# Merging laced with dense matmuls, buffers of their own for the modulation weights, gathered transposes and a root per kind of token in a hybrid attention and delta-rule block

## The chip, the cores and the metric

The kernel runs on one core of a Trainium2 chip. The metric is the device time of one execution in microseconds; before the change the median of 3 runs is 1303.28 us (1297.49 to 1310.15). Less is better.

## The reference

Two layers (`DEPTH = 2`) act on 256 latent tokens and 256 context tokens of width 1024, in 32-bit floats. Each layer computes a mixer, a residual LayerNorm, an MLP with squared ReLU, and another residual LayerNorm:

```python
sh1, sc1, g1, sh2, sc2, g2 = split((silu(c) @ w_ada[l] + b_ada[l])[:, None, :], 6)
y_lat, y_ctx = token_mixer(x_lat * (1 + sc1) + sh1, x_ctx * (1 + csc1) + csh1, w_in[l], ...)
x_lat = layer_norm(ALPHA * x_lat + g1 * y_lat, ...)
x_lat = layer_norm(ALPHA * x_lat + g2 * squared_relu_mlp(x_lat * (1 + sc2) + sh2, ...), ...)
# token_mixer: half of the width is neighbourhood attention (8 heads of 64), half gated DeltaNet (4 heads of 128)
q, k = l2norm(q), l2norm(k);  q, k = rope_2d(q), rope_2d(k);  q = q * 128 ** -0.5
# gated_delta_chunked, per chunk of tokens, head and direction
a = where(strict, (kb @ k^T) * decay, 0);  tinv = unit_lower_inverse(a)
u = tinv @ (v * beta);  w = tinv @ (kb * exp(g));  attn = (q @ k^T) * decay
v_new = u - w @ s;  o = (q * exp(g)) @ s + attn @ v_new;  s = s * cd + k_dec^T @ v_new
# gated_rmsnorm
o = o * rsqrt(mean(o * o) + 1e-6) * w * silu(z)
```

The last layer returns the latent tokens alone. `o` is linear in `q`, so a factor of the query's token can be left out of `q` and be put into `o` and into the mean of its squares.

## The kernel before

Every product with a weight is done as three matmuls of split operands (`mm3`, lines 274 to 276: hi by hi, lo by hi, hi by lo). A weight block of 128x1024 comes by DMA into a raw buffer (`wraw`, four of them), ScalarE casts it to its hi part (line 248), VectorE subtracts that from it for the lo part (line 250); three blocks are made ahead.

The modulation (adaLN) is computed in steps (`ada_steps`): each loads a block of `w_ada` into one of the same raw buffers and multiplies it by the conditioning vector in four column strips (line 301, tile `adaps`).

The mixer of a layer (`mixer`) does, in this order: four DeltaNet heads (`gdn_head`: convolution of the projected queries, keys and values, rotation, l2 norm, transposes), the gates (`gates1`, `gates2`), then per 128-token tile `t` the matrix `U` of decayed key products (line 816); eight such 128x128 matrices (two directions, four heads) per tile, 32 in all. Their unit triangular inverses are found in three stages. *Elimination:* the diagonal 32x32 blocks of all 32 matrices are brought to the layout `MY` by four strided transposes on VectorE (line 824), one sign change on ScalarE (line 825), and 30 steps of a multiplication and a subtraction on VectorE (lines 831 and 833). *Tail:* a transpose (line 834), four strided copies on ScalarE to `XT` (836) and four strided transposes on VectorE to `U` (838). *Merge:* 32x32 blocks are merged to 64x64 by the products `p1` and `pz` (lines 849 to 856), these to 128x128 by `p2` and `p3` (lines 862 to 871), in two halves of 16 matrices. The products are 32x32 and 64x64 tiles of the array. Then the scan over four token tiles and two directions follows (`scan_step`; its first product is `pvn`, line 896), and the output norm of each tile (`o_stage`).

Neighbourhood attention shares the engines: projections `N`, `K`, `Q` and `Z` (tiles `psv`, `psn`, `psz`), and `attend` (scores and values in `pss`, softmax on VectorE and ScalarE). The strings `CFG["ord0"]` and `CFG["ord1"]` give the order in which these are written for each layer: `H` a head, `B` and `C` the gates, `N K Q Z` a projection of one block, `a` one tile of attention, `f` two steps of the modulation, and `X` the place where elimination, merge and scan are written. The framework's scheduler takes instructions out of the written order by their readiness and priority, and by the buffers of each pool, so the order on an engine differs from the one written.

Of the kernel before, what the change touches and what calls it, by code (L numbers as in the profile page):

```python
# [16 lines left out]
ALU = mybir.AluOpType  # L17
# [14 lines left out]
NHOLD = 6  # L32
NB0 = 3
# [7 lines left out]
    "ord0": "HHBHHCXfNffffNNfffffNKQffaaaKaQfaaKfaQfaffaaKfaQfaZaaaZZfffafffZ",  # L41
    "ord1": "BHHHHCNfffXNfffNfNfKfQfaafKfQfaaKfQKfaQfaafffZZZaZ", "tr": 7, "tr2": 2, "acc": 2, "g": 3, "n": 3,
# [134 lines left out]
def body(ctx, tc, a, out, dump=None):  # L177
# [289 lines left out]
    def mixer(l, hT, pre, ctx_m):  # L467
# [72 lines left out]

        def gdn_head(h):
            ss = small([128, 2, 4], "gss")
            rs = small([128, 2, 4], "grs")
            tk = {}
            if last:
                V.memset(ss, 1.0)
            for kind in (0, 1):
                pt, q0 = gdn_conv(h, kind)
                tk[kind] = ktok[h] if kind == 0 else ar("qtok").rearrange("p (t c) -> p t c", t=4)
                S.activation(tk[kind][:, q0:], pt[:, q0:], AF.Copy)  # L550
                sq = ar("gsq").rearrange("p (t c) -> p t c", t=4)
                S.activation(sq[:, q0:], pt[:, q0:], AF.Square)
                V.tensor_reduce(ss[:, kind, q0:], sq[:, q0:], axis=AX.X, op=ALU.add)
                x_ = tk[kind][:, 2:4]
# [9 lines left out]
            for kind in (0, 1):  # L564
                q0 = 2 if last and kind else 0
                x_ = tk[kind][:, q0:]
                V.tensor_tensor(x_, x_, rs[:, kind, q0:].unsqueeze(2).to_broadcast([128, 4 - q0, 128]), op=ALU.mult)
                pb = sm("gtb").rearrange("p (t c) -> p t c", t=4)
                for t in range(q0, 4):
                    PE.transpose(pb[:, t], tk[kind][:, t], ident)  # L570
# [10 lines left out]
        def proj_nv(hp):  # L581
            w = getw("w_vz", l, 0, hp)
            ps = proj_T(w, 0, "psv")
# [44 lines left out]
        def gates2():  # L628
            nonlocal gc, gx, gt, cd, eg, ngc, gcb, neg, kd
            pc = sm("pc")  # L630
# [102 lines left out]
        def proj_qk(hp, kind):  # L733
            if not kind:
                biases[hp] = load_bias(hp)
            w = getw("w_na", l, 2 * hp + kind)
            t0 = 256 if (last and kind) else 0
            ps = proj_T(w, t0, "psn")
# [30 lines left out]

        def run_order(o):  # L770
            for c in o:
                if c in "fBC":
                    {"f": fill, "B": gates1, "C": gates2}[c]()
                    continue
# [33 lines left out]

        for t in ts:
# [10 lines left out]
        q4 = [slice(32 * b, 32 * b + 32) for b in range(4)]  # L820
        MY = M.tile([128, 2, 32, 32], F32, name="MY", tag="my")
        MT, Y = MY[:, 0], MY[:, 1]
        for b in range(4):
            V.transpose(MT[q4[b]], U[q4[b], :, q4[b]].rearrange("p n i -> p i n"))
# [16 lines left out]
        for t2 in range(2):  # L841
            n0 = 16 * t2
            y1 = tr("y1").rearrange("p (n c) -> p n c", n=16)
            p1 = sm("p1").rearrange("p (n c) -> p n c", n=16)
            pz = sm("pz").rearrange("p (n c) -> p n c", n=16)
            A_, B_ = [slice(64 * r, 64 * r + 32) for r in range(2)], [slice(64 * r + 32, 64 * r + 64) for r in range(2)]
            for r in range(2):
                for n in range(16):
                    PE.matmul(p1[B_[r], n], U[A_[r], n0 + n, B_[r]], XT[A_[r], n0 + n, A_[r]], start=True, stop=True)
                S.activation(y1[B_[r]], p1[B_[r]], AF.Copy)  # L850
            for r in range(2):
                for n in range(16):
                    PE.matmul(pz[A_[r], n], y1[B_[r], n], U[B_[r], n0 + n, B_[r]], start=True, stop=True)
                    PE.matmul(pz[B_[r], n], U[B_[r], n0 + n, B_[r]], y1[B_[r], n], start=True, stop=True)
                V.tensor_scalar(U[A_[r], n0:n0 + 16, B_[r]], pz[A_[r]], -1.0, None, op0=ALU.mult)
                S.activation(XT[B_[r], n0:n0 + 16, A_[r]], pz[B_[r]], AF.Copy, scale=-1.0)
            lo_, hi_ = slice(0, 64), slice(64, 128)
            for t in (2 * t2, 2 * t2 + 1):
                n0 = 8 * t
                p2 = sm("p2").rearrange("p (n c) -> p n c", n=8)  # L860
                for n in range(8):
                    PE.matmul(p2[hi_, n], U[lo_, n0 + n, hi_], XT[lo_, n0 + n, lo_], start=True, stop=True)
                y2 = tr("y2").rearrange("p (n c) -> p n c", n=8)
                S.activation(y2[hi_], p2[hi_], AF.Copy)
                p3 = sm("p3").rearrange("p (n c) -> p n c", n=8)
                for n in range(4):
                    PE.matmul(p3[lo_, n], y2[hi_, n], U[hi_, n0 + n, hi_], start=True, stop=True)
                    PE.matmul(p3[hi_, 4 + n], U[hi_, n0 + 4 + n, hi_], y2[hi_, 4 + n], start=True, stop=True)
                V.tensor_scalar(U[lo_, n0:n0 + 4, hi_], p3[lo_, 0:4], -1.0, None, op0=ALU.mult)
                S.activation(XT[hi_, n0 + 4:n0 + 8, lo_], p3[hi_, 4:8], AF.Copy, scale=-1.0)  # L870
                V.tensor_tensor(U[:, n0 + 4:n0 + 8], XT[:, n0 + 4:n0 + 8],
                                beta[:, t, 4:8].unsqueeze(2).to_broadcast([128, 4, 128]), op=ALU.mult)
        if l == 0:
            dump("LT", U)
# [46 lines left out]
        def o_stage(t):  # L921
# [45 lines left out]
        for step in range(4):  # L967
            for d in range(2):
                scan_step(step, d)
# [148 lines left out]
    P0.tile([128, 40], F32, name="pad")  # L1118
# [194 lines left out]
```

## Time and profile before

| | |
|---|---|
| median of 3 runs | 1303.28 us (1297.49 to 1310.15) |
| the profiled execution | 1304.05 us, span 1302.3 us |
| mean granted clock of TensorE | 0.963 |
| busy: TensorE, its weight loads, VectorE, ScalarE, GpSimd | 95%, 77%, 67%, 46%, 6% of the span |

The profile gives an engine's busy time in a stretch, the time of one instruction by line and shape, what ended an engine's idle time, and the granted clock as a share of 2.4 GHz (0.50 is 1.2 GHz). A matmul's record is longer than the distance to the next one, since matmuls are pipelined. A 32-bit matmul of small tiles leaves two records per instruction.

### The profile page before, as it was taken

To read this page: it belongs to the slowest core of one execution; us is meant where nothing else is said; L and a number is where in the kernel's file an instruction comes from. 1 tells how busy PE (TensorE), PEld (TensorE's weight loads), DVE (VectorE), ACT (ScalarE), POOL (GpSimd) and SP (SyncE) were. 2 spreads that over 40 slices of the span, in tenths; PEclk is the share of its full clock that TensorE was granted. 3 is DMA by queue.
4 is the path that set the end of the run, shared out by engine and by line. 5 is a ranking of instruction groups with operands and counts; after the bars stand their busy time and mean duration, and the time that the engine had idled before them with its cause. 6 is when DMAs were issued, how large, how long until landed. Compare 5 with 4: busy or idle time off the path is not lost.

```text
span 1302.3 us, 20475 instructions
## 1 busy us (share of the span) xinstructions
PE 1234.8 (95%) x7976; PEld 1006.3 (77%) x7976; DVE 875.1 (67%) x1681; ACT 604.6 (46%) x1079; POOL 81.6 (6%) x82
## 2 busy tenths in 40 slices
PE   7999998999999999999999999899979998999997
PEld 3676666988878988777788888675669877788996
DVE  3788695466579955344444488897965668866677
ACT  2554545565555732322322455555454655544552
POOL 0212100001001000000000001221000010000000
PEclk9999995899999999999999999999958999899999
DMA  9613661023255643533532256235720256555552
GB/s 329 213 65 102 211 219 46 17 78 117 79 194 182 225 150 109 165 130 115 164 129 99 97 178 204 72 107 191 235 92 14 85 179 231 199 184 191 186 187 98
DMA packets 62721, 190.93 MB, mean 147 GB/s; under 512 B 7808, under 2 KB 17824, under 8 KB 62624
## 3 DMA queue, kind: packets, MB, share of 16 engines
q1 hardware_dynamic: 62624, 189.62, 44.2%
q8 instruction: 63, 1.03, 0.3%
q14 instruction: 34, 0.28, 0.1%
HBM read 187.46 MB, written 2.13 MB: 146 GB/s over the span
## 4 chain that ended last, share of the span: by engine, by line
PE 71%; DVE 11%; ACT 4%; issue 2%; POOL 1%; DMA 1%; DVEq 0%; ACTq 0%; POOLq 0%
PE pst L274 7%; PE pst L276 7%; PE pst L275 7%; PE pm L274 7%; PE pm L276 7%; PE pm L275 7%; PE pss L716 3%; PE adaps L301 2%; DVE wlo L250 2%; PE pss L696 2%; PE pss L713 2%; PE psn L274 1%; PE psn L275 1%; PE psn L276 1%; ACT XT L836 1%
## 5 line engine op out<-in xcount | busy, mean ns | idle before, releaser
L250 DVE TENSOR_TENSOR wlo<-wraw,whi 128x1024 fp32r<-128x1024 f32 x224 | 274.7, 1228 | 184.7 <-ACT whi L248 184.3
L248 ACT ACTIVATE whi<-wraw 128x1024 fp32r<-128x1024 f32 x224 | 237.0, 1060 | 316.6 <-PE pst L276 168.9
L274 PE MATMUL pm<-hhi,whi 128*128 128x256 f32 (+1 forms) x544 | 176.4, 324 | 0.8 <-ACT whi L248 0.7
L276 PE MATMUL pm<-hhi,wlo 128*128 128x256 f32 (+1 forms) x544 | 174.5, 321 | 0.0
L275 PE MATMUL pm<-hlo,whi 128*128 128x256 f32 (+1 forms) x544 | 174.4, 321 | 0.0
L274 PE MATMUL pst<-whi,ah 128*128 128x512 f32 x384 | 150.0, 391 | 0.0
L275 PE MATMUL pst<-wlo,ah 128*128 128x512 f32 x384 | 149.5, 389 | 0.0
L276 PE MATMUL pst<-whi,al 128*128 128x512 f32 x384 | 149.1, 389 | 0.0
L274 PEld LDWEIGHTS pm<-hhi,whi 128*128 128x128 f32 x544 | 103.5, 190 | 14.4 <-issue 5.8
L276 PEld LDWEIGHTS pm<-hhi,wlo 128*128 128x128 f32 x544 | 103.6, 190 | 7.7
L275 PEld LDWEIGHTS pm<-hlo,whi 128*128 128x128 f32 x544 | 103.6, 190 | 7.3
L274 PEld LDWEIGHTS pst<-whi,ah 128*128 128x128 f32 x384 | 72.1, 188 | 15.6 <-issue 0.8
L276 PEld LDWEIGHTS pst<-whi,al 128*128 128x128 f32 x384 | 72.1, 188 | 14.8
L275 PEld LDWEIGHTS pst<-wlo,ah 128*128 128x128 f32 x384 | 72.1, 188 | 14.7
L274 PE MATMUL psg<-hhi,whi 128*128 128x512 f32 (+1 forms) x216 | 78.2, 363 | 4.6 <-ACT XT L529 2.3
L276 PE MATMUL psg<-hhi,wlo 128*128 128x512 f32 (+1 forms) x216 | 78.0, 362 | 0.2 <-DVE wlo L250 0.2
L275 PE MATMUL psg<-hlo,whi 128*128 128x512 f32 (+1 forms) x216 | 77.8, 361 | 0.0
L531 DVE SCALAR_TENSOR_TENSOR XT<-U,cw,XT 128x512 f32<-128x512 f32 (+1 forms) x96 | 66.9, 728 | 0.5 <-ACT XT L529 0.4
L1191 ACT ACTIVATE ah<-mr 128x256 fp32r<-128x256 f32 (+1 forms) x68 | 33.5, 492 | 65.6 <-DVE mr L1189 65.6
L301 PE MATMUL adaps<-wraw,scT 128*32 128x256 f32 x640 | 56.0, 397 | 4.8 <-DMA wraw<-w_ada 4.6
L229 POOL TENSOR_TENSOR rs<-ve,mh 128x1 f32<-128x1 f32 x12 | 12.5, 1044 | 629.3 <-DVE bmv L394 362.2
L1192 DVE TENSOR_TENSOR al<-mr,ah 128x256 fp32r<-128x256 f32 (+1 forms) x68 | 35.2, 518 | 24.3 <-ACT ah L1191 24.2
(659 smaller groups left out, 2467.4 us busy)
## 6 DMA issues: line engine op xcount, KB each, us to landing
wraw<-w SPq DMA_DIRECT2D x140, 512.0 KB
wraw<-w_ada SPq DMA_DIRECT2D x80, 512.0 KB
wraw<-w_gdn SPq DMA_DIRECT2D x27, 512.0 KB
wraw<-w_out SPq DMA_DIRECT2D x24, 512.0 KB
xa<-w_ada SPq DMA_DIRECT2D x32, 256.0 KB
wraw<-w_vz SPq DMA_DIRECT2D x16, 512.0 KB
wraw<-w_na SPq DMA_DIRECT2D x16, 512.0 KB
lnrow<-lnr SPq DMA_DIRECT2D x8, 512.0 KB
```

The costliest lines, as they stand in the source:

```text
L248: S.activation(hi, r, AF.Copy)
L250: V.tensor_tensor(lo, r, hi.bitcast(F32), op=ALU.subtract)
L274: PE.matmul(o, l[0], r[0], start=start, stop=False)
L275: PE.matmul(o, l[0], r[1], start=False, stop=False)
L276: last_mm[:] = [PE.matmul(o, l[1], r[0], start=False, stop=stop).ins]
L301: PE.matmul(st["ps"][32 * g:32 * g + 32, :256], scT[:, k, :], w[:, 256 * g:256 * g + 256], start=(k == 0), stop=(k == 7), tile_position=(0 ...
L531: V.scalar_tensor_tensor(av, cin[:, sg:, kk:kk + 256], cw[:, b, kk:kk + 1], av, op0=ALU.mult, op1=ALU.add)
L696: PE.matmul(ps[:, :128 * nkt], nqT[hp][:, a2, qs], nkT[hp][i][:, a2, :128 * nkt], start=i == 0, stop=i == 1)
L713: PE.transpose(ps[:, 128 * kt_:128 * kt_ + 128], p_[:, 128 * kt_:128 * kt_ + 128], ident)
L716: PE.matmul(ps[:, 0:65], p_[:, 128 * kt_:128 * kt_ + 128], nv[:, kt_, hd], start=kt_ == 0, stop=kt_ == nkt - 1)
L1191: S.activation(ah, r, AF.Copy)
L1192: V.tensor_tensor(al, r, ah.bitcast(F32), op=ALU.subtract)
```

## The change

1. **Laced merging.** The merge becomes a function in which TensorE's order is as written. p1 of both quadrants alternates, and so does pz; p2 of two tiles come together, then p3 of both. After each of these eight groups three dense steps are written, of three matmuls each, out of three projection blocks that follow `Y` in the order string. All of attention is written behind `S`, the scan.
2. **Own raw buffers.** The modulation weights go to the tile `wada`, two buffers, and no longer to `wraw`.
3. **Gathered transposes.** ScalarE gathers the diagonal blocks, 32x8x32 at a time, so that one VectorE transpose does for four. In the tail a second whole transpose and four strided copies, two on VectorE and two on ScalarE, take the place of the four strided transposes to `U`.
4. **Key root.** Queries and keys get a reciprocal root each. The keys are multiplied by theirs as before; the queries' is kept (`rq`, and its square `rq2`) and enters the output norm.
5. The order strings, and the size of an unused tile (`pad`).

```diff
 CFG = {
-    "ord0": "HHBHHCXfNffffNNfffffNKQffaaaKaQfaaKfaQfaffaaKfaQfaZaaaZZfffafffZ",
-    "ord1": "BHHHHCNfffXNfffNfNfKfQfaafKfQfaaKfQKfaQfaafffZZZaZ", ...
+    "ord0": "HHBHHCXfNffNffNffKffYQNKSffffffaaaaQfaaKfaQfaffaaKfaQfaZaaaZZfffafffZ",
+    "ord1": "BHHHHCNfffXNffNffKffQfYNKQSfffaaffaafKfQKfaQfaafffZZZaZ", ...
...
-            w = wraw(a["w_ada"][l, 128 * k:128 * (k + 1), 1024 * n:1024 * (n + 1)])
+            w = P0.tile([128, 1024], F32, name="wada", tag="wada", bufs=2)
+            SP.dma_start(w, a["w_ada"][l, 128 * k:128 * (k + 1), 1024 * n:1024 * (n + 1)])
...
-            V.tensor_scalar(ss, ss, 4 * NORM_EPS, None, op0=ALU.add)
-            rsq(rs, ss, mh.rearrange("p (a b) -> p a b", a=2))
-            V.tensor_scalar(rs[:, 1], rs[:, 1], 128.0 ** -0.5, None, op0=ALU.mult)
...
-                V.tensor_tensor(x_, x_, rs[:, kind, q0:].unsqueeze(2).to_broadcast([128, 4 - q0, 128]), op=ALU.mult)
+                if kind == 0:
+                    V.tensor_tensor(x, x, rs.unsqueeze(2).to_broadcast([128, 4, 128]), op=ALU.mult)
+                else:
+                    V.tensor_scalar(rq[:, q0:, h], rs[:, q0:], 128.0 ** -0.5, None, op0=ALU.mult)
...
+        def dense(o):
+            end = None
+            for c in o:
...
+                for k in range(KT):
+                    mm3(ps[:, t0:], (w[0][:, 128 * k:128 * k + 128], w[1][:, 128 * k:128 * k + 128]),
+                        (hT[0][:, k, t0:], hT[1][:, k, t0:]), k == 0, k == KT - 1)
+                    if k == LACE - 1 and end:
+                        end()
+                    yield
...
+            for b in range(4):
+                S.activation(Y[q4[b], :, 8 * t:8 * t + 8].rearrange("p i n -> p n i"), U[q4[b], 8 * t:8 * t + 8, q4[b]], AF.Copy)
...
-        for b in range(4):
-            V.transpose(MT[q4[b]], U[q4[b], :, q4[b]].rearrange("p n i -> p i n"))
+        V.transpose(MT, Y)
...
+        V.transpose(MT, Y)
         for b in range(4):
-            V.transpose(U[q4[b], :, q4[b]].rearrange("p n i -> p i n"), Y[q4[b]])
+            o, i = U[q4[b], :, q4[b]].rearrange("p n i -> p i n"), MT[q4[b]]
+            V.tensor_copy(o, i) if b % 2 else S.activation(o, i, AF.Copy)
...
+        def merge(work):
+            def chunk():
+                for _ in range(LACE):
+                    next(work, None)
...
+            with tc.manual_schedule(engines={nc.tensor.engine}):
+                for t2 in range(2):
...
+                    for n in range(16):
+                        for r in range(2):
+                            PE.matmul(p1[r][B_[r], n], U[A_[r], n0 + n, B_[r]], XT[A_[r], n0 + n, A_[r]], start=True, stop=True)
+                    for r in range(2):
+                        S.activation(y1[B_[r]], p1[r][B_[r]], AF.Copy)
+                    chunk()
...
+            V.tensor_tensor(ss, ss, rq2[:, t], op=ALU.mult)
             V.tensor_scalar(ss, ss, 1.0 / 128, NORM_EPS, op0=ALU.mult, op1=ALU.add)
             rsq(rs, ss, mh[:, 0:4])
+            V.tensor_tensor(rs, rs, rq[:, t], op=ALU.mult)
```

TensorE ahead of pz in layer 0. Before (`adaps` modulation, `p` the tile p1, `pss` attention, `psn` a K or Q projection):

```order
L276 MATMUL psn<-hhi,wlo 128x512
L301 MATMUL adaps<-wraw,scT 32x256
L849 MATMUL p_1309<-XT,U 32x32 x16
L301 MATMUL adaps<-wraw,scT 32x256 x7
L849 MATMUL p_1309<-XT,U 32x32 x16
L853 MATMUL pz<-U,y_1308 32x32
```

The same place in the change:

```order
L882 MATMUL p_1617<-XT,U 32x32
L882 MATMUL p_1616<-XT,U 32x32
L882 MATMUL p_1617<-XT,U 32x32
L276 MATMUL psn<-hhi,whi 128x512
L277 MATMUL psn<-hlo,whi 128x512
L278 MATMUL psn<-hhi,wlo 128x512
L276 MATMUL psn<-hhi,whi 128x512
L277 MATMUL psn<-hlo,whi 128x512
L278 MATMUL psn<-hhi,wlo 128x512
L276 MATMUL psn<-hhi,whi 128x512
L277 MATMUL psn<-hlo,whi 128x512
L278 MATMUL psn<-hhi,wlo 128x512
```

The two quadrants of p1, one after the other before, alternate, and nine matmuls of the laced projection stand between p1 and pz.

VectorE from the end of the elimination of layer 0 on. Before (`MY` the elimination's tile, `KL` and `QS` split keys and queries of attention, `ob` its output):

```order
L834 STREAM_TRANSPOSE MY<-MY 128x1024
L838 STREAM_TRANSPOSE U<-MY 32x32x32 x4
L755 TENSOR_TENSOR KL<-psn,KS 64x512
L719 TENSOR_SCALAR ob<-pss,arc 128x64 x2
L755 TENSOR_TENSOR KL<-psn,KS 64x512
L855 TENSOR_SCALAR U<-pz 32x16x32
```

In the change:

```order
L858 STREAM_TRANSPOSE MY<-MY 128x1024
L861 STREAM_TRANSPOSE MY<-MY 128x1024
L864 COPY U<-MY 32x32x32 x2
L892 TENSOR_SCALAR U<-pz 32x16x32 x2
L252 TENSOR_TENSOR wlo<-wraw,whi 128x1024
```

The attention operations are gone from between; a second transpose stands behind the first, and two copies in the place of four transposes.

ScalarE at the same place, before:

```order
L836 ACTIVATE XT<-MY 32x32x32 x4
L850 ACTIVATE y_1308<-p_1309 32x512
L744 ACTIVATE QS<-psn 64x512
L248 ACTIVATE whi<-wraw 128x1024
L850 ACTIVATE y_1308<-p_1309 32x512
```

In the change:

```order
L860 ACTIVATE XT<-MY 32x32x32 x4
L884 ACTIVATE y_1615<-p_1616 32x512
L884 ACTIVATE y_1615<-p_1617 32x512
L864 ACTIVATE U<-MY 32x32x32 x2
L893 ACTIVATE XT<-pz 32x16x32 x2
```

The two copies of p1's results stand together, ahead of the two copies to `U` that ScalarE got.

## Rows read from the trace of the kernel before

**Rows 1.** The page: busy time of each engine; costliest groups (line, engine, operation).

```profile
PE 1234.8 (95%) x7976; PEld 1006.3 (77%) x7976; DVE 875.1 (67%) x1681; ACT 604.6 (46%) x1079; POOL 81.6 (6%) x82
...
L274 PE MATMUL pst<-whi,ah 128*128 128x512 f32 x384 | 150.0, 391 | 0.0
```

**Rows 2.** Stages of layer 0: stretch, length, busy PE, PEld, DVE, ACT, POOL, clock, DMA, GB/s.

```profile
49.70:117.70 68.00, 60.57 (x297) 47.32 (x295) 59.83 (x115) 35.99 (x62) 15.38 (x17) 0.97 0.23 76
...
132.40:160.30 27.90, 27.90 (x186) 18.53 (x185) 19.00 (x28) 15.61 (x45) 3.51 (x1) 1.00 0.60 193
160.30:193.30 33.00, 30.53 (x185) 21.42 (x185) 30.95 (x81) 12.29 (x19) 0.00 (x0) 1.00 0.67 225
193.30:206.00 12.70, 7.78 (x88) 5.18 (x87) 12.01 (x10) 11.09 (x9) 0.00 (x0) 0.72 0.36 122
206.00:242.00 36.00, 36.00 (x512) 30.50 (x510) 13.36 (x35) 13.37 (x28) 0.00 (x0) 0.58 0.06 16
242.00:372.60 130.60, 128.34 (x890) 108.63 (x886) 79.18 (x233) 76.35 (x191) 13.19 (x11) 1.00 0.25 79
```

**Rows 3.** The same by stage, layer 1.

```profile
812.00:884.20 72.20, 62.65 (x369) 49.59 (x367) 63.70 (x141) 38.67 (x74) 17.53 (x20) 0.98 0.34 110
...
910.10:944.20 34.10, 31.05 (x221) 22.72 (x222) 30.93 (x85) 14.37 (x23) 0.00 (x0) 1.00 0.70 227
944.20:956.80 12.60, 5.06 (x88) 3.96 (x88) 11.80 (x11) 10.96 (x9) 0.00 (x0) 0.73 0.46 160
956.80:991.20 34.40, 34.40 (x514) 29.47 (x511) 14.39 (x36) 13.60 (x26) 1.83 (x1) 0.60 0.09 29
991.20:1079.90 88.70, 86.29 (x661) 74.80 (x660) 55.71 (x161) 48.05 (x118) 7.57 (x8) 0.98 0.33 106
```

**Rows 4.** The same, a stretch within the merge of layer 0.

```profile
205.00:233.10 28.10, 28.10 (x386) 24.14 (x383) 10.48 (x23) 10.28 (x20) 0.00 (x0) 0.50 0.07 21
```

**Rows 5.** Groups of instructions on GpSimd (count, busy, mean, idle before).

```profile
L229 POOL TENSOR_TENSOR grs<-gss,mh 128x8 f32<-128x8 f32 x8 | 16.1, 2007 | 7.9 <-DVE gss L561 7.9
```

**Rows 6.** Groups on VectorE, 117 to 245 us.

```profile
L250 DVE TENSOR_TENSOR wlo<-wraw,whi 128x1024 fp32r<-128x1024 f32 x10 | 12.2, 1220 | 1.1 <-ACT whi L248 1.0
L824 DVE STREAM_TRANSPOSE MY<-U 32x1024 f32<-32x1024 f32 x4 | 8.0, 2012 | 0.1
L755 DVE TENSOR_TENSOR KL<-psn,KS 64x512 fp32r<-64x512 f32 x8 | 5.5, 687 | 0.2
```

**Rows 7.** Waits in the heads of layer 0 (total, times, longest).

```profile
DVE grs L563 <- POOL grs L229: 4.6, 3, 1.6
```

**Rows 8.** Groups on ScalarE, 117 to 245 us.

```profile
L805 ACT ACTIVATE dec<-gcr,gcb 128x128 f32<-128x128 f32 x32 | 8.9, 401 | 3.7 <-PE gcr L801 3.7
L836 ACT ACTIVATE XT<-MY 32x1024 f32<-32x1024 f32 x4 | 7.8, 1950 | 1.0 <-DVE MY L834 1.0
```

**Rows 9.** Tile psn (dense projection) alone: stretch, length, busy PE, PEld, DVE, ACT, clock.

```profile
190.00:195.90 5.90, 5.90 (x25) 4.60 (x25) 1.36 (x2) 2.36 (x4) 1.00 0.27 92
```

**Rows 10.** Windows of the tiles p (p1, then p2 and p3) alone.

```profile
198.00:199.30 1.30, 1.25 (x32) 1.11 (x32) 0.00 (x0) 0.00 (x0) 0.88 0.00 0
217.20:219.70 2.50, 2.46 (x32) 2.27 (x32) 0.42 (x1) 0.00 (x0) 0.50 0.00 0
241.40:242.10 0.70, 0.68 (x16) 0.54 (x16) 0.00 (x0) 0.00 (x0) 1.00 0.00 0
```

**Rows 11.** Windows of the tile pz alone.

```profile
211.10:213.10 2.00, 1.92 (x64) 1.78 (x64) 0.00 (x0) 0.00 (x0) 0.50 0.00 0
233.70:235.00 1.30, 1.20 (x64) 1.09 (x64) 0.00 (x0) 0.00 (x0) 1.00 0.00 0
```

**Rows 12.** Windows of the tile pss (attention) alone, behind the start of each scan.

```profile
242.00:372.60 130.60, 46.50 (x296) 38.13 (x296) 25.91 (x91) 24.59 (x52) 1.00 0.25 79
991.20:1079.90 88.70, 23.82 (x151) 18.83 (x151) 13.10 (x41) 10.96 (x22) 0.98 0.33 106
```

**Rows 13.** Window of the tile adaps (modulation) alone.

```profile
132.40:206.00 73.60, 13.38 (x150) 4.24 (x150) 0.84 (x2) 0.00 (x0) 0.95 0.59 195
```

More of the change, by code (lines that the diff above doesn't have):

```diff
@@ L32 @@
 NHOLD = 6
+LACE = 3
+NLACE = 3
 NB0 = 3
@@ L539, in gdn_conv @@
             return pt, q0
+        rq = P0.tile([128, 4, 4], F32, name="rq", tag="rq")
+        rq2 = P0.tile([128, 4, 4], F32, name="rq2", tag="rq2")
         def gdn_head(h):
[L542 to L546, printed above, removed]
             for kind in (0, 1):
                 pt, q0 = gdn_conv(h, kind)
-                tk[kind] = ktok[h] if kind == 0 else ar("qtok").rearrange("p (t c) -> p t c", t=4)
-                S.activation(tk[kind][:, q0:], pt[:, q0:], AF.Copy)
+                x = ktok[h] if kind == 0 else ar("qtok").rearrange("p (t c) -> p t c", t=4)
+                S.activation(x[:, q0:], pt[:, q0:], AF.Copy)
                 sq = ar("gsq").rearrange("p (t c) -> p t c", t=4)
                 S.activation(sq[:, q0:], pt[:, q0:], AF.Square)
-                V.tensor_reduce(ss[:, kind, q0:], sq[:, q0:], axis=AX.X, op=ALU.add)
-                x_ = tk[kind][:, 2:4]
+                ss, rs = small([128, 4], "gss", bufs=4), small([128, 4], "grs", bufs=4)
+                V.tensor_reduce(ss[:, q0:], sq[:, q0:], axis=AX.X, op=ALU.add)
+                V.tensor_scalar(ss[:, q0:], ss[:, q0:], 4 * NORM_EPS, None, op0=ALU.add)
+                rsq(rs[:, q0:], ss[:, q0:], mh[:, q0:4])
+                x_ = x[:, 2:4]
                 ra = ar("rope")[:, :256].rearrange("p (t c) -> p t c", t=2)
@@ L560, in gdn_head @@
                 V.tensor_tensor(x_, x_, ra, op=ALU.add)
-            V.tensor_scalar(ss, ss, 4 * NORM_EPS, None, op0=ALU.add)
-            rsq(rs, ss, mh.rearrange("p (a b) -> p a b", a=2))
-            V.tensor_scalar(rs[:, 1], rs[:, 1], 128.0 ** -0.5, None, op0=ALU.mult)
-            for kind in (0, 1):
-                q0 = 2 if last and kind else 0
-                x_ = tk[kind][:, q0:]
-                V.tensor_tensor(x_, x_, rs[:, kind, q0:].unsqueeze(2).to_broadcast([128, 4 - q0, 128]), op=ALU.mult)
+                if kind == 0:
+                    V.tensor_tensor(x, x, rs.unsqueeze(2).to_broadcast([128, 4, 128]), op=ALU.mult)
+                else:
+                    V.tensor_scalar(rq[:, q0:, h], rs[:, q0:], 128.0 ** -0.5, None, op0=ALU.mult)
                 pb = sm("gtb").rearrange("p (t c) -> p t c", t=4)
                 for t in range(q0, 4):
-                    PE.transpose(pb[:, t], tk[kind][:, t], ident)
+                    PE.transpose(pb[:, t], x[:, t], ident)
                 S.activation(kqT[h][:, kind].rearrange("p (t c) -> p t c", t=4)[:, q0:], pb[:, q0:], AF.Copy)
@@ L768, in mixer @@
         cnt2 = dict.fromkeys("NKQZaH", 0)
+        def dense(o):
+            end = None
+            for c in o:
+                i = cnt2[c]
+                cnt2[c] += 1
+                w = getw(*(("w_vz", l, 0, i) if c == "N" else ("w_na", l, 2 * i + "KQ".index(c))))
+                ps = acc("psv" if c == "N" else "psn")
+                t0 = 256 if last and c == "Q" else 0
+                for k in range(KT):
[4 more added lines that the diff above has]
+                    yield
+                end = (lambda i=i, ps=ps: proj_nv(i, ps)) if c == "N" else (lambda i=i, c=c, ps=ps: proj_qk(i, "KQ".index(c), ps))
+            end()
         def run_order(o):
+            o = iter(o)
             for c in o:
-                if c in "fBC":
-                    {"f": fill, "B": gates1, "C": gates2}[c]()
+                if c == "Y":
+                    merge(dense([next(o) for _ in range(NLACE)]))
+                    continue
+                if c in "fBCS":
+                    {"f": fill, "B": gates1, "C": gates2, "S": lambda: scan()}[c]()
                     continue
@@ L807, in decay @@
             return D_
+        q4 = [slice(32 * b, 32 * b + 32) for b in range(4)]
+        MY = M.tile([128, 2, 32, 32], F32, name="MY", tag="my")
+        MT, Y = MY[:, 0], MY[:, 1]
         for t in ts:
@@ L965, in o_final, with scan @@
             to_mix(of, 4, 4, t)
-        for step in range(4):
-            for d in range(2):
-                scan_step(step, d)
+        def scan():
+            for step in range(4):
+                for d in range(2):
+                    scan_step(step, d)
         obt = M.tile([128, 16, 2, 64], F32, name="ob", tag="my")
@@ L1117, in body @@
     late_const()
-    P0.tile([128, 40], F32, name="pad")
+    P0.tile([128, 56], F32, name="pad")
     dump("h0", hT[0].bitcast(F32))
```

86 lines of the change are left out of this document (44 added, 42 removed).

## The prediction

> **What bounds the kernel now.** The profiled execution took 1304.05 us, its span is 1302.3 us, and the runs shown have a median of 1303.28 us, so the sum below is made against 1304.05 and 0.8 us come off at the end. I read the page's busy times first: TensorE is busy for 95% of the span [rows 1], so on the whole only what TensorE leaves idle or runs at a lower clock can be won. An average hides where that is, so the next view is the busy time by stage, with the stages of the gated DeltaNet cut at the marks of the timeline. In layer 0 [rows 2] the six rows are the heads, the gates to the start of the elimination, the elimination, its tail up to the first pz matmul, the merge up to the start of the scan, and the scan with attention. The reader is to see three things. In the heads TensorE idles for 68.0 - 60.6 = 7.4 us. In the elimination VectorE is busy for 30.95 of 33.0 us: VectorE sets its end. In the merge TensorE is busy all 36 us, but at a granted clock of 0.58. Layer 1 shows the same [rows 3]: 9.6 us idle in its heads, 30.9 of 34.1 us of VectorE, a clock of 0.60. The clock's own row says that from 205.0 to 233.1 us it was 0.50 throughout, TensorE never idle [rows 4]: the lower level, 1.2 GHz, after a tail in which TensorE had worked 7.8 of 12.7 us on small tiles.
>
> **The change part by part**, by stage, first layer 0.
>
> *Heads.* One root of 128x8 on GpSimd (2.0 us, [rows 5]) for queries and keys together becomes two of 128x4; the key's can start before the queries are convolved. One 128x512 product per head (about 0.69, [rows 6], a 64x512 product) goes, and two small additions come in its place. VectorE waited 4.6 us for that root [rows 7], and TensorE's idle 7.4 us lie around it. Bounds: 0, if VectorE's own 59.8 of 68 us set the pace, and -7.4. I take -5, two thirds, since both the wait and part of VectorE's work go.
>
> *Gates to elimination.* The four strided transposes of 2.0 us (8.0 in all, [rows 6]) go. In their place stand 16 ScalarE gathers of 32x256 and one whole transpose (2.0, the same 1024 elements per partition). A gather is bounded by a 128x128 activation, 0.40, and a quarter of a strided 32x1024 one, 1.95/4 = 0.49 [rows 8]; I take 0.40. Twelve of them, 4.8 us, fall between the 32 exponentials, where ScalarE is busy for 15.6 of 27.9 us [rows 2]; I let 1.8 show. The last four (1.6) and the transpose lie open. -8.0 + 1.8 + 1.6 + 2.0 = -2.6, say -2.5; with all twelve hidden -4.4, with none +0.4.
>
> *Elimination.* Its 60 small operations stay. The new order leaves one lo product in it instead of five, four KL instead of six and no QS instead of two. A lo product is 1.22, a KL 0.69 (QS the same shape) [rows 6]: 4 x 1.22 + 4 x 0.69 = 7.6. I take -7, since the softmax operations that go and the casts that stay nearly cancel. What was done there is late: see the last step.
>
> *Tail.* p1 now needs all four strided copies to XT (4 x 1.95 = 7.8, [rows 8]); before, it started after two. Then a second transpose on VectorE (2.0), which waits for these copies because it writes the tile they read, and two VectorE copies that pz needs. Their price is not in the trace: 0.69 below, 1.95 above; I take 1.22, a VectorE pass over 1024 elements [rows 6]. 2.0 + 7.8 + 2.0 + 2.4 = 14.2, with handovers 15 against 12.7: +2.3; bounds +1.2 and +3.8.
>
> *Merge.* After each of eight groups of small matmuls stand nine 512-column ones, 72 in all. Nine lie before pz. 25 such matmuls took 5.9 us [rows 9], 0.23 each, so the 63 others take 14.5 at the full clock. The small ones, by records (two to an instruction): 64 left of p1 at 1.25/32 [rows 10], 256 of pz at 1.20/64 [rows 11], 128 of p2 and p3 at 0.68/16 [rows 10]: 2.5 + 4.8 + 5.4 = 12.7. Together 27.2. Ahead of p1 the new order takes some 21 us of work from TensorE (the displaced work below) and shortens that stretch by less, so TensorE idles there and the clock will be low at p1; I let it come back within the first dense runs and add 2.8. 30 against 36: -6.
>
> Skill against row here: the records of pz, which write two column strips in turn, cost 0.019 each, those of p1 in one strip 0.039 [rows 10, 11]. So p1, whose two quadrants now alternate, should halve, 2.5 us a layer; I take -2. The Trainium skill, "TensorEngine Tiling (Array Packing)", Key Properties, says that different tiles can execute in parallel, which this row bears out, and also that changing the tiling mode drains TensorE, which speaks against lacing. What a switch costs at most the rows say: a 512-column matmul takes 0.39 [rows 1] where its successor follows after 0.23, so 0.16 at each of 16 switches, 2.6 us a layer; by that rule the sum would be 5 us higher, 1304.
>
> *Displaced work.* The start of the scan moves by -5 - 2.5 - 7 + 2.3 - 6 = -18.2. But less of the other work is done by then: in the new order 44 attention matmuls, 40 of the projections and 32 of the modulation stand behind the scan's start that stood ahead of it. At 46.5/296 = 0.157 [rows 12], 0.23 and about 0.15 (two records of at most 0.089, [rows 13]) that is 6.9 + 9.2 + 4.8 = 20.9. Behind the scan's start TensorE is busy for 128.3 of 130.6 us [rows 2], so nothing covers it: +21. Layer 0: +2.8.
>
> Layer 1 in the same steps, from [rows 3]: heads -5 of 9.6; gates 0 (this stage is 2 us shorter there, so the gathers show); elimination -7; tail +2.4 (15 against 12.6); merge 30 against 34.4, -4.4. Scan's start -14. Displaced are 45 attention matmuls at 23.8/151 = 0.158 [rows 12] and 12 of the projections: 7.1 + 2.8, with the handovers 10.5; TensorE is busy for 86.3 of 88.7 us there. Layer 1: -3.5.
>
> Costed at nothing: the modulation weights' own two buffers (their loads and products lie where TensorE is busy anyway; the price if it must wait for a load is a microsecond or two at each); two small VectorE operations in each of six output norms, off the path while attention fills TensorE; the MLP and the start, which are unchanged.
>
> Sum: +2.8 - 3.5 - 4 (p1 in both layers) = -4.7, so 1299.4, and 0.8 off: about **1299 us**, no change that can be told: a measurement of this kernel tells about 1%, 13 us.
>
> **The rivals.**
>
> *Faster: the idle goes, too.* If all of the heads' idle goes (-2.4 and -4.6 beyond my terms), the gathers hide (-2 and -4), the tail stays at 12.7 (-2.3 twice) and the clock is full at once in the merge (-2.8 twice), the time is 1299 - 23 = 1276; half of that is 1287. For it: every one of these is a bound that the rows allow, and the wait of VectorE shows that the heads hang on that root. Against it: the displaced work stays, and TensorE's 95% leave 67 us of idle time over the whole span. I take 1284 for it, chance 0.33.
>
> *Slower: the clock stays low in the laced merge.* The rows show 28 us in a row at 0.50 while TensorE was busy without a gap [rows 4]; what it did were small tiles with three to five dense matmuls between. In the new order the small tiles stay, and TensorE comes from a longer idle time. At the lower level the 63 dense matmuls take 29 (twice 14.5), pz 256 x 1.92/64 = 7.7 [rows 11], p2 and p3 128 x 2.46/32 = 9.8 [rows 10], p1 about 5: 51 instead of 30, 21 us a layer, 1341. It decides from the point where it holds for more than about half of both merges: then the 1% is passed. Against it: nine dense matmuls stand together now, and in the last 2 us before the scan the clock was full (p2 and p3 ran at 0.68 for 16 records, [rows 10]). The Trainium skill, "TensorE: Matmul & The Clock Gate", Part 1, says that the slow clock is the default and that activity releases it; whether this mixture is activity enough no run here shows. Chance 0.12.
>
> *Slower: the new order waits.* All of attention now stands behind the scan's start, where softmax on VectorE and ScalarE must follow each score block, and VectorE has 21 us a layer less slack; if its chain lets TensorE idle for a tenth of that stage (0.1 x 220 = 22 over both layers, against 4.7 now), and the switches cost the 5 us above, 1299 + 17 + 5 = 1321; half of it 1310. Chance 0.13, taken at 1317.
>
> *The change doesn't do it.* If the merge's clock is set by something later and the heads by VectorE alone, terms and counter-terms shrink together: 1304, not to be told from the forecast.
>
> **Numbers.** Forecast with the last rival 0.42, at 1299, its own range 1290 to 1310; faster 0.33; low clock 0.12; order 0.13. Faster by over 1% (under 1290): 0.33. Slower by over 1% (over 1316): the low clock and some three quarters of the last, 0.21. Within: 0.46. The range leaves out the low clock beyond half of both merges and the deepest part of the faster case: 1275 to 1322.
>
> **What would show it.** Right: in the windows of the new profile, elimination near 26 us, tail near 15, merge near 30 with a granted clock above 0.8 and p1's 64 records in a run in about the time that 32 take now; scan's start 18 and 14 us earlier, and a scan stage longer by 21 and 10. Wrong: a merge at 0.5 for more than half of its length; idle time of TensorE behind the scan's start put down to softmax; waits for the root as long as before; a tail that ends on the second transpose or on a copy of over 2 us. The forecast falls most easily on the displaced work: if attention behind the scan runs beside the scan's own waits better than 98% busy suggests, the gain of 18 and 14 us remains.

## The result, and the profile after

The changed kernel takes 1315.46 us (1313.43 to 1318.32, 8 runs) against 1303.68 us (1297.16 to 1310.36, 8 runs): a ratio of 1.0097, with a 95% interval from 1.0068 to 1.0125. It is slower by about 1%; 1299 was forecast. Executions more than 1.5% above the fastest of their kernel are left out of every ratio. The profiled execution of the changed kernel has a span of 1315.1 us, 12.8 more than before.

The page's line that answers to [rows 1]:

```profile
PE 1222.9 (93%) x7976; PEld 983.0 (75%) x7976; DVE 852.2 (65%) x1683; ACT 631.6 (48%) x1115; POOL 85.4 (6%) x90
```

TensorE left as many records in 11.9 us less busy time (in the two merges alone, at the full clock now, 19.5 us less), and idled for 92.2 us in place of 67.5. So more was lost to idle time than won by the clock. The windows by stage say where. Layer 0, columns as in [rows 2]; the first row is the heads with the stage behind them up to the first product of the gates, then gates, elimination, tail, merge, scan:

```profile
49.30:125.00 75.70, 70.50 (x364) 53.74 (x364) 70.14 (x141) 44.96 (x78) 23.00 (x25) 1.00 0.31 107
125.00:156.90 31.90, 29.45 (x170) 18.06 (x169) 13.43 (x28) 25.48 (x60) 3.51 (x1) 1.00 0.50 159
156.90:183.20 26.30, 9.76 (x66) 4.66 (x64) 24.02 (x70) 4.30 (x7) 0.00 (x0) 0.72 0.53 177
183.20:196.40 13.20, 5.66 (x73) 4.49 (x73) 5.23 (x4) 11.01 (x8) 0.00 (x0) 0.53 0.01 1
196.40:223.40 27.00, 26.37 (x516) 21.26 (x516) 10.74 (x17) 13.71 (x21) 0.00 (x0) 1.00 0.13 41
223.40:379.60 156.20, 154.25 (x1047) 124.14 (x1045) 92.44 (x274) 87.98 (x213) 13.30 (x11) 1.00 0.31 100
```

Layer 1, from the gates on, beside [rows 3]:

```profile
888.20:919.70 31.50, 29.37 (x185) 17.63 (x183) 12.26 (x26) 25.66 (x61) 3.51 (x1) 1.00 0.58 183
919.70:949.00 29.30, 15.60 (x119) 7.29 (x118) 25.80 (x72) 5.28 (x9) 0.00 (x0) 0.72 0.72 235
949.00:962.90 13.90, 9.48 (x100) 5.38 (x100) 5.71 (x5) 11.68 (x8) 0.00 (x0) 0.50 0.51 149
962.90:987.40 24.50, 24.50 (x520) 20.66 (x520) 10.28 (x19) 12.64 (x20) 0.00 (x0) 0.99 0.13 46
987.40:1090.50 103.10, 97.98 (x731) 84.97 (x730) 65.14 (x197) 57.06 (x138) 9.39 (x9) 0.98 0.28 90
```

The reader is to see four things. The merge has the full clock now, 1.00 and 0.99 where it was 0.58 and 0.60. In the elimination VectorE still sets the pace, but TensorE works 9.8 of 26.3 us, where it worked 30.5 of 33.0. The gates' stage, which the change was to shorten in layer 0, is longer: ScalarE is now busy in it for 25.5 of 31.9 us and VectorE for 13.4. And the scan stage is 25.6 us longer, TensorE busy in it all but 2 us: it does there what it did not do in the elimination.

With the same marks in both traces (the elimination from its first operation behind the transposes to the transpose behind it, so that it begins and ends up to 0.5 us off the rows above) the stages compare so (us; "forecast" is the change that the prediction's steps gave, with p1's 2 us in the merge):

| stage | layer 0: before, after | change (forecast) | layer 1: before, after | change (forecast) |
|---|---|---|---|---|
| to the gates | 83.7, 75.7 | -8.0 (-5) | 72.2, 69.2 | -3.0 (-5) |
| gates | 27.8, 31.9 | +4.1 (-2.5) | 25.8, 31.5 | +5.7 (0) |
| elimination | 33.6, 26.3 | -7.3 (-7) | 34.7, 29.3 | -5.4 (-7) |
| tail | 12.2, 13.2 | +1.0 (+2.3) | 12.1, 13.9 | +1.8 (+2.4) |
| merge | 36.0, 27.0 | -9.0 (-8) | 34.4, 24.5 | -9.9 (-6.4) |
| scan | 130.6, 156.2 | +25.6 (+21) | 88.7, 103.1 | +14.4 (+10.5) |

With 0.6 ahead of the heads and 2.2 behind the last scan that makes +12.8.

### The profile page after: what moved, and what is told of

The parts are those of the page before. It is cut to its first block, busy times and chain, and to the rows that moved or that the text cites. A ratio compares the mean times of both kernels' runs of the same rounds, so it can differ in the third digit from the quotient of the medians.

```text
span 1315.1 us, 20510 instructions
## 1 busy us (share of the span) xinstructions
PE 1222.9 (93%) x7976; PEld 983.0 (75%) x7976; DVE 852.2 (65%) x1683; ACT 631.6 (48%) x1115; POOL 85.4 (6%) x90
## 4 chain that ended last, share of the span: by engine, by line
PE 74%; DVE 11%; ACT 7%; issue 2%; POOL 2%; DMA 0%; DVEq 0%; ACTq 0%; POOLq 0%
PE pst L276 8%; PE pst L277 8%; PE pst L278 8%; PE pm L276 7%; PE pm L278 7%; PE pm L277 7%; PE pss L718 3%; PE adaps L304 3%; DVE wlo L252 2%; PE psn L276 2%; PE psn L277 2%; PE psn L278 2%; PE pss L698 1%; DVE XT L534 1%; PE pss L715 1%
## 5 line engine op out<-in xcount | busy, mean ns | idle before, releaser
L276 PEld LDWEIGHTS pm<-hhi,whi 128*128 128x128 f32 x544 | 103.6, 190 | 14.4 <-issue 5.8
L304 PE MATMUL adaps<-wada,scT 128*32 128x256 f32 x640 | 64.3, 417 | 19.7 <-DMA wada<-w_ada 19.6
L304 PEld LDWEIGHTS adaps<-wada,scT 128*32 128x32 f32 x640 | 16.7, 112 | 49.5 <-DMA wada<-w_ada 28.3
L231 POOL TENSOR_TENSOR rs<-ve,mh 128x1 f32<-128x1 f32 x12 | 12.2, 1018 | 631.0 <-DVE bmv L397 362.2
```

Source lines behind the costliest of these rows:

```text
L231: G.tensor_tensor(outp, x, m, op=ALU.pow)
L276: PE.matmul(o, l[0], r[0], start=start, stop=False)
```

## Experiments

All times are medians, all ratios are against the kernel before on the same chip. The runs were spread over several chips, and the kernel before has medians from 1298.4 to 1305.6 us on them, so a difference of two runs' times carries a few us of doubt.

**1. The key root alone** (`e1_root`): the kernel before with part 4 of the change.

> The kernel before with the key root alone (a root per kind, the queries' factor in the output norm); all else as before. The heads of the changed kernel were 4.9 us (layer 0) and 2.6 us (layer 1) shorter up to the gates. If the root did that, this kernel is about 7 us faster than before, 1296 to 1297, in the heads alone, and elimination, tail and merge stay at 33, 13 and 36 us. Rival: the heads were shorter because the modulation's loads no longer share the raw buffers with the weights; then this kernel is within 2 us of before.

1287.29 us, ratio 0.9871 (0.9815 to 0.9926). More than either expectation. Up to the gates layer 0 is 6.1 us shorter (77.6), layer 1 0.7 (71.5). Most of the rest is in the merge of layer 0, whose row reads (the merge of layer 1 below it):

```profile
198.00:222.50 24.50, 24.11 (x534) 20.32 (x530) 15.98 (x36) 16.51 (x31) 0.00 (x0) 1.00 0.27 88
942.50:976.90 34.40, 34.40 (x512) 29.47 (x509) 14.29 (x36) 13.55 (x26) 1.82 (x1) 0.60 0.10 29
```

Nothing in the merge was changed, and it has the full clock in layer 0: 11.5 us less. The timeline of TensorE ahead of it (start, length, instruction) shows what is different:

```profile
190.46 1.19 PE L848 MATMUL p<-XT,U 32*32 32x32 f32 x32 [1.03 <-ACT XT L835]
...
192.16 0.63 PE L274 MATMUL psn<-hhi,whi 128*128 128x512 f32 x1
...
194.72 0.55 PE L274 MATMUL psn<-hhi,whi 128*128 128x512 f32 x1
195.10 0.39 PE L275 MATMUL psn<-hlo,whi 128*128 128x512 f32 x1
...
197.12 1.10 PE L848 MATMUL p<-XT,U 32*32 32x32 f32 x29 [0.47 <-ACT y L849]
```

Between the two halves of p1 the scheduler now happened to have a projection: its matmuls are 0.63 long at the lower clock and 0.39 from 195.1 on. In layer 1 and in the kernel before, nothing dense stands there, and the clock stays at 0.50 into the merge [rows 4]. What stands within the merge hardly differs: 15 records of projections, 44 of attention and 16 of the modulation here, 16, 40 and none in the kernel before. So the two merges of layer 0 did nearly the same work, one at 1.00 and one at 0.58; they differ in the clock with which they were entered.

**2. Without the gathers** (`e2_nogather`):

```diff
-            for b in range(4):
-                S.activation(Y[q4[b], :, 8 * t:8 * t + 8].rearrange("p i n -> p n i"), U[q4[b], 8 * t:8 * t + 8, q4[b]], AF.Copy)
...
-        V.transpose(MT, Y)
+        for b in range(4):
+            V.transpose(MT[q4[b]], U[q4[b], :, q4[b]].rearrange("p n i -> p i n"))
```

> The changed kernel with the four strided transposes ahead of the elimination in place of the 16 gathers and the one transpose; the tail as changed. Theory of the gathers (they are the loss): about 12 us faster than the changed kernel, 1303. Theory of the moved work (TensorE idles in elimination and tail, and the work that stood there comes back behind the scan's start): only what the stage from the gates to the elimination was longer than before comes back, 1.5 and 5.3 us, so about 1308 to 1309, and the scan stages stay at 156 and 103 us.

1310.38 us, ratio 1.0057 (1.0028 to 1.0085): 5 us of the 12, near what the theory of the moved work had (6 to 7). The gates' stages take 28.2 and 28.2 us, the scan stages stay at 156.9 and 103.1. In layer 0 the gates are back (27.8 before). In layer 1 they are still 2.4 us longer than before, so that part of its +5.7 is not the gathers'; the key root alone (experiment 1) has 27.6 us there.

**3. Shared raw buffers** (`e3_wraw`): the modulation's load as before.

> The changed kernel with the modulation's blocks in the shared raw buffers again. Theory of the buffers (two are too few: TensorE waited 19.6 us for these loads, 4.6 before): 8 to 12 us faster than the changed kernel, about 1305. Theory of the moved work: those waits lie in elimination and tail, where TensorE has no other work; 0 to 3 us, about 1314.

1316.83 us, ratio 1.0093 (1.0066 to 1.012): no difference, so the two buffers are not the loss. Whether the waits are is not shown by this run: TensorE waited 17.1 us for the modulation's loads here too, 19.6 in the changed kernel and 4.6 before. That they cost little because TensorE has no other work there stays argued.

**4. The order strings of before, with the laced merge** (`e4_fill`):

```diff
-    "ord0": "HHBHHCXfNffNffNffKffYQNKSffffffaaaaQfaaKfaQfaffaaKfaQfaZaaaZZfffafffZ",
-    "ord1": "BHHHHCNfffXNffNffKffQfYNKQSfffaaffaafKfQKfaQfaafffZZZaZ", ...
+    "ord0": "HHBHHCXfNffffNNfffffNKQffaaaaYKQKSffaaaafQfaafaaKfQfaffaZaaZZfffffffffZ",
+    "ord1": "BHHHHCNfffXNfffNfNfKfQfaaYKQKSffaaffQfaafKfQaafffffZZZZ", ...
```

> The changed kernel with its order strings alone changed: projections, modulation and the first attention tiles stand ahead of the merge as in the kernel before, and the laced blocks are the three that follow (K, Q, K). Theory of the moved work: TensorE is busy over 85% of elimination and tail again, the scan stages shrink from 156 and 103 us to about 130 and 90, the scan starts 6 to 12 us later for the softmax in the elimination, and the merge keeps a clock above 0.8: about 1290 to 1300, below both kernels. Theories of gathers or buffers: within 4 us of the changed kernel, 1311 to 1319.

1300.34 us, ratio 0.998 (0.9951 to 1.0008): 15 us below the changed kernel, with nothing altered but the order. It met the upper end expected and is not below the kernel before. Elimination, merge and scan of layer 0:

```profile
155.40:190.80 35.40, 30.59 (x188) 18.21 (x188) 28.44 (x78) 10.23 (x17) 0.00 (x0) 0.87 0.76 245
205.80:242.20 36.40, 35.30 (x578) 28.86 (x578) 19.79 (x50) 21.02 (x37) 1.82 (x1) 1.00 0.10 31
242.20:368.20 126.00, 123.80 (x846) 103.22 (x844) 76.78 (x229) 73.27 (x186) 10.48 (x10) 1.00 0.26 82
```

TensorE's work in the elimination is back (30.6 us), the scan stage is 30 us shorter than in the changed kernel, and the scan starts 19 us later. Half of those 19 us are the elimination, 9.1 us longer; the other half is the merge, 36.4 us in place of 27.0 at the full clock, since 64 attention records stand in it now. The exchange is worth 11 us in this layer: what TensorE does in the elimination's gaps need not be done behind it. In layer 1 it comes to less than 1 us over the layer: the scan stage is 15.8 us shorter there, elimination and merge 8.2 and 9.1 longer.

**5. One run in place of eight** (`e5_first`): the same 72 matmuls, 24 behind the first p1 and 48 behind the last group.

> The changed kernel with its 72 laced matmuls placed otherwise: 24 of them (one whole block) behind the first p1, the other 48 behind the last group of the merge; the seven other gaps of the merge are bare. Theory of the single run (what raises the clock is one run of dense matmuls in the tail, and the merge keeps it then): the granted clock stays above 0.9 in the merge, which waits somewhat for its own copies, 27 to 31 us in layer 0 and 25 to 29 in layer 1; the time 1315 to 1322. Theory of the lacing (dense matmuls are needed in every gap): the clock falls to 0.50 in the bare part and the merge takes 33 us or more; 1325 or more.

1337.71 us, ratio 1.0253 (1.0215 to 1.0291). The theory of the single run fell. In the merge:

```profile
199.80:205.00 5.20, 2.19 (x137) 2.07 (x137) 3.97 (x5) 3.31 (x5) 0.00 (x0) 0.76 0.30 104
205.00:210.00 5.00, 4.81 (x77) 4.50 (x77) 0.79 (x2) 1.56 (x3) 0.00 (x0) 0.50 0.01 3
210.00:215.00 5.00, 3.66 (x182) 3.25 (x178) 1.74 (x4) 1.55 (x3) 0.00 (x0) 0.50 0.01 3
```

The first p2 of the merge on the timeline of TensorE, with the idle time before it:

```profile
204.11 3.35 PE L902 MATMUL p<-XT,U 64*64 64x64 f32 x29 [3.01 <-ACT XT L895]
```

Bare, the groups wait for their own copies (TensorE 2.2 of 5.2 us busy, 3.0 us idle in a row ahead of p2), the clock falls to 0.50, and the merge takes 35.4 us against 27.0. So this merge needs other work between its groups. Whether the clock is held by that work or only by the absence of the idle time, the run doesn't tell apart.

**6. One laced block on the kernel before with the key root** (`e6_lace1`): `NLACE = 1`, all eight steps behind the first p1, and the order strings of before with `YKS` in them.

> The kernel before with the key root, as in the first experiment, and with one laced block alone (24 dense matmuls behind the first p1 of each layer; order strings of before, attention mostly where it was; strided transposes, tail and raw buffers of before). There the merge of layer 0 had the full clock (24.5 us) and that of layer 1 had 0.60 (34.4 us). Theory of the single run: layer 1's merge gets the full clock as well, with the block in it about 28 us, and its tail no idle 8 us: 8 to 12 us faster than the first experiment, 1275 to 1279. If lacing is needed in every gap, or the manual order costs what it gives: 1285 to 1292.

1294.46 us, ratio 0.9924 (0.9901 to 0.9946): 7 us slower than the first experiment, both expectations missed. The merges are at 1.00 and 0.84 of the clock, 20.8 and 21.0 us long, but the tails grew from 11.7 and 12.0 to 21.9 and 21.9, as the whole block lies in them at the lower clock at first. Tail and merge together are 6.5 us longer than in the first experiment in layer 0 and 3.5 shorter in layer 1, so the rest of the 7 us lies elsewhere and stays open.

**7. Gathers on VectorE** (`e7_vgather`): `V.tensor_copy` for `S.activation` in the gather.

> The changed kernel with its 16 gathers a layer on VectorE in place of ScalarE. On ScalarE a gather took 0.66 us, 2.7 for four ahead of the next tile's exponentials; VectorE copied 32x1024 in 1.06, so a quarter should take about 0.3, and it idles for 16 of 29 us there. Theory of the gathers: the stage from the gates to the elimination shrinks by 5 to 7 us in each layer, and since the elimination has idle TensorE time all of it reaches the end: 1302 to 1306. Theory that only the moved work counts: 1311 or more.

1307.41 us, ratio 1.0043 (1.0021 to 1.0066): 8 us below the changed kernel, against 5 for taking the gathers away. The gates' stages take 23.1 and 24.0 us, 8.8 and 7.5 less, but only half of that reaches the end, where all of it was expected to: the elimination is 3.7 and 1.1 us longer, for one. One gather, on ScalarE in the changed kernel, and on VectorE here:

```profile
L844 ACT ACTIVATE MY<-U 32x256 f32<-32x256 f32 x16 | 10.5, 658 | 0.4 <-DVE U L842 0.3
```

```profile
L844 DVE COPY MY<-U 32x256 f32<-32x256 f32 x16 | 6.2, 389 | 0.3
```

**8 and 11. One laced block, gathers on VectorE, split tail** (`e8_lace1_vg_split`, and again as `e11_lace1_again`): the sixth kernel, with the gathers of the seventh, the changed kernel's tail, and in it

```diff
-            S.activation(XT[q4[b], :, q4[b]].rearrange("p n i -> p i n"), MT[q4[b]], AF.Copy)
+            o, i = XT[q4[b], :, q4[b]].rearrange("p n i -> p i n"), MT[q4[b]]
+            V.tensor_copy(o, i) if b else S.activation(o, i, AF.Copy)
```

> The second kernel of this call (key root, one laced block, order of before) with the gathers on VectorE and one transpose ahead of the elimination, and in the tail three of the four copies to XT on VectorE (1.06 each) and one on ScalarE. TensorE is busy nearly throughout there, so what is saved on VectorE and ScalarE, about 6 us a layer ahead of the elimination and 3 in the tail, comes back in part as work behind the scan's start. If half of it stays: 1266 to 1272. If TensorE is all that counts: the same as the second kernel within 3 us.

> The eighth run's kernel again, beside the other two on one chip: 1274 to 1279.

1275.97 us, ratio 0.9787 (0.9759 to 0.9816), and again 1275.48, 0.9821 (0.9797 to 0.9845): 18 us below the sixth kernel, as much as the expectation had the chain lose (6 and 3 us a layer) and not the half (the level that was expected was too low, since the sixth run's was), and 40 below the changed one. The fastest version of this study. Its layer 0 from the gates on:

```profile
126.00:150.10 24.10, 24.10 (x136) 15.90 (x136) 18.15 (x42) 14.70 (x43) 3.51 (x1) 1.00 0.55 182
150.10:181.70 31.60, 29.20 (x194) 18.55 (x192) 26.81 (x73) 8.59 (x14) 0.00 (x0) 0.95 0.71 227
181.70:200.10 18.40, 13.41 (x114) 10.38 (x114) 12.85 (x18) 11.55 (x14) 0.00 (x0) 0.81 0.30 111
200.10:224.80 24.70, 24.39 (x514) 19.32 (x513) 14.45 (x38) 14.99 (x29) 0.00 (x0) 1.00 0.13 40
```

TensorE is fed in the elimination and the merge has the full clock; both hold in layer 1 as well. Only the first of the merge's gaps is laced by the program; in the others the scheduler put 23 records of projections and 42 of attention. So a block in every gap is not needed for the clock.

**9. The same without lacing** (`e9_root_vg_split`): order and merge of the kernel before.

> The kernel before (its order, its merge, nothing laced) with the key root, the gathers on VectorE with one transpose, and three of the four copies to XT on VectorE: the best of the second call without its laced block. Theory that the laced block brings the clock: without it one merge at least is at 0.6 again, 8 to 11 us slower than the laced one, 1284 to 1288. Theory that the shorter tail keeps TensorE busy enough by itself: both merges at a clock above 0.9, and the time 1266 to 1274, below the laced one, since the manual order of the merge cost 7 us in the sixth run.

1288.28 us, ratio 0.99 (0.9869 to 0.9931). That is the median of twelve runs. The ten of them that the ratio uses have 1286.3, 11 us above the laced kernel on the same chip, as the first theory had it. They go from 1277.94 us, at a mean granted clock of 0.981, to 1293.96, at 0.967, and on the whole the time falls as the clock rises; the six of the laced kernel lie within 4.7 us. In its profile the merge of layer 0 has 0.99 and that of layer 1 0.61.

**10. All parts kept, three repairs** (`e10_vg_split_fill`): the changed kernel with the order of the fourth run, VectorE gathers and the split tail.

> All four parts of the change kept (three laced blocks, own buffers, gathers, key root), with three repairs: the order strings of the fourth run (attention and projections ahead of the merge), gathers on VectorE, three copies to XT on VectorE. The fourth run had 1300; the gathers gave 8 in the seventh, the split tail shortens the tail by about 4 a layer: 1284 to 1290 if they add. If TensorE's work is the bound by then, 1290 to 1297. Three laced blocks against one (the eighth run, 1276): they pull 33 us of matmuls ahead of the scan that fit better behind it, so above 1276 by all theories.

1279.54 us, ratio 0.9853 (0.9827 to 0.9879): 36 us below the changed kernel (32 by the ratios, as the chips differ), and 5 better than expected. With three laced blocks it is 4 us above the version with one.

**12. The key root alone, again** (`e12_root_again`).

> The first experiment's kernel (key root alone on the kernel before) again, in more rounds. In its profile the merge of layer 0 had the full clock by one run of projections between the two halves of p1, that of layer 1 had 0.60. If that is where its 16 us came from, 11 of them depend on the clock: the times spread over 10 us or more, and fall with each run's granted clock; median 1286 to 1296. If the root itself is worth 16 us, the times agree within 5 us, as in the first four runs, at 1286 to 1290.

1288.34 us, ratio 0.9885 (0.9842 to 0.9928); the times agree within 4.9 us, so the spread that was expected of the clock is not there, and by that test the root itself would be worth the 16 us. The stages of both profiles say otherwise: against the kernel before 6.1 us lie ahead of the gates of layer 0, and 11.5 and 9.3 in its merge. The projection stands between the halves of p1 in both, at the full clock, but here TensorE idled for 2.0 us behind it, the merge began at 0.50 and was back at 1.00 from 205 us on: 0.88 in all, 26.7 us. The merge of layer 1 has 0.66. Why the times agree all the same stays open, as do some 4 us that both profiles gain behind the last scan (218.6 against 222.4).

## Why the prediction was wrong, point by point

- **Heads: right in kind.** -8.0 and -3.0 for -5 and -5. The root alone gives -6.1 and -0.7 (experiment 1). TensorE's waits for the key's tile (`ktok`, ahead of `gtb`) fell from 12.6 to 3.2 us over both layers, and to 3.1 with the root alone.
- **Gates to elimination: the failed step.** The prediction took 0.40 for a gather, with 0.49 as its bound, and let 1.8 us of twelve show. A gather took 0.66, beyond the bound: the nearest rows [rows 8] were a contiguous activation and a quarter of a longer strided one, and the shorter one did not scale down with its elements. All sixteen, 10.5 us, lay in the chain that VectorE waits for: +4.1 and +5.7 in place of -2.5 and 0. VectorE's waits for the exponentials behind the gathers, in the gates of layer 0, before and after (total, times, longest):

```profile
DVE U L816 <- ACT dec L805: 3.9, 6, 2.3
DVE U L842 <- ACT dec L828: 13.0, 8, 5.3
```

  Without the gathers the stages are 3.7 and 3.2 us shorter though 6.8 us of transposes are back in them (experiment 2), so some 10 us of gathers show in each layer. Of layer 1's +5.7, 2.4 us remain without them. Experiment 7 takes the stages below those of before.
- **Elimination, tail: right** within 2 us each. The whole transpose took 1.25 for 2.0, and a VectorE copy 1.07 for 1.22. One reading was off: p1 does not wait for all four copies to `XT`, nor did its start wait for two of them before. It started after the first one then (198.00; the copy ended at 197.94), and went on after the third in the change (191.05; 191.00).
- **Merge: right, and better than the term.** Clock 1.00 and 0.99. p1's 62 records took 1.91 us at the lower clock, where 32 took 1.9 before: alternating quadrants do halve it. The Trainium skill, "TensorEngine Tiling (Array Packing)", Key Properties, says that different tiles run in parallel; the trace agrees with that number. Its drain at a change of mode was bounded at 2.6 us a layer in the prediction. The merge as a whole came out below the sum without a drain, 27.0 for 28, but the starts of the matmuls around a group show a price:

```profile
199.48 0.39 PE L277 MATMUL psn<-hlo,whi 128*128 128x512 f32 x1
199.71 0.39 PE L278 MATMUL psn<-hhi,wlo 128*128 128x512 f32 x1
200.03 2.08 PE L900 MATMUL p<-XT,U 64*64 64x64 f32 x32
202.03 0.50 PE L276 MATMUL psn<-hhi,whi 128*128 128x512 f32 x1
202.37 0.39 PE L277 MATMUL psn<-hlo,whi 128*128 128x512 f32 x1
```

  Dense matmuls start 0.23 apart; the group starts 0.32 behind the last of them, and behind the group the second starts 0.34 after the first. That is some 0.1 us a switch, an estimate of 1.6 us for the 16 switches of a layer, within the bound. Whether it is that drain, no run tells apart. What the sum had too much of was the return of the clock, 2.8 us: it came back ahead of the merge, which ran at 1.00 and 0.99. The rival of the low clock was a true mechanism for another kernel (experiment 5): bare groups, with 3.0 us of idle time among them, fell to 0.50; with nine dense matmuls in each gap the clock stayed at 1.00. The Trainium skill, "TensorE: Matmul & The Clock Gate", Part 1, says that activity releases the slow clock; both runs agree with it, but the 28 us at 0.50 in which TensorE was busy without a gap [rows 4] do not, if busy time is activity.
- **Displaced work: the step that decides, and mis-sized.** That it comes back at the end is shown by experiment 4, where the scan stages are 30.2 and 15.8 us shorter. Its size was 20.9 and 10.5; the stages grew by 25.6 and 14.4. For attention the prediction divided a busy time by records [rows 12] and multiplied by instructions: 296 records in layer 0 are 212 instructions, 0.22 us each and not 0.157. Attention behind the scan's start in the changed kernel, in layer 0 and in layer 1:

```profile
223.40:379.60 156.20, 54.38 (x352) 44.81 (x352) 32.87 (x112) 29.51 (x64) 1.00 0.31 100
987.40:1090.50 103.10, 34.15 (x212) 27.04 (x212) 18.17 (x58) 16.41 (x32) 0.98 0.28 90
```

  That is 7.9 and 10.3 us more than in [rows 12], where the prediction had 6.9 and 7.1. In layer 0 the projections were the larger error. They were priced at 0.23, as in a run [rows 9]; behind the scan's start they take, before and after:

```profile
242.00:372.60 130.60, 23.89 (x80) 14.26 (x80) 8.24 (x12) 7.10 (x12) 1.00 0.25 79
223.40:379.60 156.20, 38.01 (x121) 20.91 (x120) 12.38 (x18) 10.61 (x18) 1.00 0.31 100
```

  That is 14.1 us more for 41 records more, 0.34 each, mixed with other work, where the prediction had 9.2. The modulation took 6.7 us more (6.54 to 13.26) for 4.8. Since records overlap, these three exceed the 25.6. In layer 1 the projections took 1.3 us more for 2.8, and 2.7 us of the growth are idle time.
- **The rival of the new order** is not what happened: TensorE is busy for 154.3 of 156.2 us in the scan stage of layer 0. It does more there; it does not wait. In layer 1 it idles 5.1 us for 2.4. That the rival's 1317 is near the time measured is chance.
- **The chances.** The gates' two errors make 12.3 us and the scan stages' two 8.5, against some 5 us that the merges gave beyond the forecast: with these two stages as measured the sum of -4.7 would have been +16, 3 us from the 12.8 between the profiles. The range held the time, but a gain of a few us was forecast and a loss of 12 came.

Taken together: the key root on the kernel before is worth 15 to 16 us, so beside it the other parts as put together here cost 27 to 28. The two numbers do not stand for parts that add up: 9 to 11 of the root's us lie in the merge of layer 0, which ran at 1.00 and 0.88 of the clock in the two profiles, and lacing gives the full clock there, too. The changed kernel without the root was not run, so what the root is worth in it stays open. Of what the other parts cost, the new order is 15 (experiment 4; 11 of it in layer 0) and ScalarE's gathers 8 (experiment 7), measured one at a time on the changed kernel.

## What to carry to other kernels

Work that is taken from under a long chain on another engine, to fill a later stage, leaves a hole in the busiest engine: count the hole first, then the gain. Where a stage's clock depends on what happens to stand ahead of it, one block of dense work there can give it the full clock (experiments 8 and 11); whether that steadies the time is not settled, as the sixth kernel, laced too, spread over 10.5 us, and the twelfth, not laced, over 4.9. And price a moved instruction by the rows of the place it goes to, records by records or instructions by instructions, never one by the other.

## What was not expected of the hardware

VectorE was the faster engine for strided copies: 0.39 us for 32x256 against 0.66 on ScalarE, 1.07 for 32x1024 against 1.93 to 1.98. A whole 128x1024 transpose took 1.25 us from a contiguous tile and 1.91 from a strided one. Halving the root's elements on GpSimd, 128x8 to 128x4, brought 2.0 us to 1.29 only. And ten runs of one unlaced program (experiment 9) differed by 16 us, on the whole in step with the mean granted clock, 0.966 to 0.981.
